# A hybrid decoder block: load order at the start, gate rows on ScalarE, selectors ahead, products of some pairs exchanged

## The chip, the cores and the metric

The kernel runs on one core of one Trainium2 chip. The metric is the device time of one execution in microseconds; the time of a kernel is the median of its runs. One execution is also taken by the hardware profiler, and all rows below are from it. Engines: PE is TensorE, DVE VectorE, ACT ScalarE, POOL GpSimd, and SP issues most of the transfers.

## The reference, cut to what matters

A block with 512 tokens and 16 meta tokens (528 columns, NT), 1024 channels, float32. Two mixers read the same normed input; learned gates merge them; a SwiGLU follows.

```
xn   = rmsnorm(h) * g1
proj = xn @ w_in           # mq mk mv mi mf mo | gq gk gv ga gr | gate_m gate_g
mq, mk = silu(causal conv of width 4)
hm   = mLSTM in chunks of 64, 4 heads: weights exp(b_t - b_s + i_s - m_t), from gates mi, mf
y_m  = headnorm(hm) * sigmoid(mo)
y_g  = headnorm(gated linear attention of gq gk gv) * silu(gr)
h   += (sigmoid(gate_m) * (y_m @ W_m) + sigmoid(gate_g) * (y_g @ W_g)) @ W_out
h   += (silu(hn @ Wfg) * (hn @ Wfu)) @ Wdown,   hn = rmsnorm(h) * g2
out  = rmsnorm(h) * gf
```

## The kernel before, in words

Everything lies transposed: channels on the 128 partitions, tokens in the columns. A *unit* is one block of 128 output channels: its weights, 128 x 1024 (512 KB), come from DRAM into a tile `raw` (4 buffers, L183) and are split into a high part on ScalarE (`whi`, L190) and the rest on VectorE (`wlo`, L195). x is split in the same way, and every product is three matmuls, high x high, high x low, low x high (`mm3`, L304 to L306). A unit is 8 k-steps over the input channels. Where it needs all 528 columns, a k-step is two halves of 264 columns, six matmuls.

The order of the work is the order in which the code is traced; each engine works through its own queue in that order. All small work is in Python generators. `run` puts one into the list `side`, `mix` into the list `mixers`; after each k-step `tick` takes each generator in `side` one step further, and of `mixers` the first alone. So the heads of the mLSTM run one after another, a head's generator begins where the one ahead ends, and `yield n` waits n ticks. PSUM has 8 banks, taken by `bank()`; a product into a bank waits until its last reader is done.

`begin` issues the load five units ahead, and it puts the splits of later units into the current one's k-steps by a table (PLAIN for a unit, FIRST and SECOND for a pair).

The order of units is: gates, mq 0; a sum of squares over all channels (L1091) and from it `rstd` (`rsqrt_mean`); mk 0, mv 0, mv 1, mo 0, mo 1, mq 1, mk 1, mv 2 and so on, 24 units to 191 us. Up to mv 1 products use x without its norm, and `rstd` is multiplied in where a bank is read. `normed_x` writes the normed x meanwhile.

`gate_rows` (L629) starts with the k-steps of mk 0. On 32 partitions it makes the log gates, running sums and maxima (a scan, L660), the four groups of rows `R`, and for each distance d of two chunks a row (ten adds with one scalar per partition, L685). These are transposed (L701) into a bank and copied to `acol` (L695), and then `ready` lets the heads of the mLSTM begin. A head (`mlstm`, L878) copies its selector (L883) and lets six ticks pass. Two products with `R` spread the head's rows over all partitions (L886 and the one before it). Then come scores, exponentials and weights for each chunk of keys.

From 191 us many units are taken as *pairs*: two blocks of outputs with x in quarters, seven products in place of eight (`pair`, L351). A pair forms seven products p7, q1, p3 (that of the pair before), q6, p4, p2, q5 of four k-steps each into three banks:

```
        seven(bz, w, x, "p7", True, hook, *cols)
        seven(bx, w, x, "q1", True, hook, *cols)
        if "p3" in pend:
            pend.pop("p3")(hook)
```

q1 and q6 go into the same bank, and between them the copy `s1` (L406 here, L1391 in the gate/up pairs) reads q1 from it; `s7` (L409) reads p7 from its bank. Both are issued at the first k-step of p3; where no p3 is pending, that is right behind q1. Such a pair follows single units: gm 0, gq 0, and the first of 16 gate/up pairs. `s2` adds two halves of a raw tile (L229) and releases it. A tick follows every second k-step of a pair.

At the end `final` (L1487) sums the squares of the outputs, takes Ln and Exp on ScalarE, refines the result on VectorE in four operations (L1501 to L1504) and scales the outputs.

Of the kernel before, what the change touches and what calls it, by code (L numbers as in the profile page):

```python
# [8 lines left out]
F32 = mybir.dt.float32  # L9
# [93 lines left out]
def hybrid_block(ctx: ExitStack, tc: tile.TileContext, xT, wst, par, con, out):  # L103
# [5 lines left out]
    def nm(s):  # L109
        cnt[0] += 1  # L110
        return f"{s}_{cnt[0]}"
# [86 lines left out]
    def split_hi(u):  # L198
        splits[u] = [whi(raws[u])]

    def split_lo(u):
        splits[u].append(wlo(raws.pop(u), splits[u][0]))
# [54 lines left out]
    def g_lo(u):  # L257
# [6 lines left out]

    PLAIN = {"s": [(split_hi, 2), (split_lo, 4)], "e": [(e_hi, 1), (e_lo, 3), (s2, 4)],
             "a": [(a_hi, 1), (a_lo, 3), (f_hi, 4), (s4, 5)]}
    FIRST = {"s": [(split_hi, ("q1", 2)), (split_lo, ("p3", 1))],
             "e": [(e_hi, ("q1", 2)), (e_lo, ("p3", 1)), (s2, ("q6", 1))]}
    SECOND = {"s": [(split_hi, ("p2", 0)), (split_lo, ("p2", 2))],
              "a": [(a_hi, ("p2", 0)), (a_lo, ("p2", 2)), (f_hi, ("q5", 0)), (s4, ("q5", 2))],  # L270
              "e": [(e_hi, ("p2", 0)), (e_lo, ("p2", 2)), (s2, ("q5", 2))]}
# [79 lines left out]
    def pair(names, x, cols, sink):  # L351


        u, steps = begin(*names)
        w = mixw[u].w
        bz, bx, by = (bank()[:, :cols[1] - cols[0]] for _ in range(3))
        e = sink(bz, bx, by)
        todo = {("p7", 0): ["s5"], ("p7", 2): ["mid", "c22"], ("q6", 0): ["c12"], ("q6", 2): ["fin"]}
        mine = {("p3", 0): ["s1", "s7"], ("p4", 0): ["s2"], ("p2", 1): ["c21"], ("q5", 0): ["c11"]}
        steps.setdefault(("p7", 3), []).append(lambda: f_lo(u))  # L360
        steps.setdefault(("q6", 1), []).append(lambda: g_hi(u))
        steps.setdefault(("p4", 1), []).append(lambda: g_lo(u))

        def hook(n, k):
            left(*todo.get((n, k), ()))
            for s in mine.get((n, k), ()):
                e.pop(s)()
            for f in steps.get((n, k), ()):
                f()
            if k % 2:  # L370
                tick()

        seven(bz, w, x, "p7", True, hook, *cols)
        seven(bx, w, x, "q1", True, hook, *cols)
        if "p3" in pend:
            pend.pop("p3")(hook)
        else:
            for k in range(4):
                hook("p3", k)
        seven(bx, w, x, "q6", False, hook, *cols)  # L380
        seven(bz, w, x, "p4", False, hook, *cols)
        seven(by, w, x, "p2", True, hook, *cols)
        seven(bx, w, x, "q5", False, hook, *cols)
        assert not pend, pend
        pend.update(e)
        pend["p3"] = lambda hook=lambda n, k: None: seven(bx, mixw.pop(u).w, x, "p3", False, hook, *cols)
# [29 lines left out]
        return sink  # L416


    pr = cpool.tile([P, NPAR], F32, name="pr")
    nc.sync.dma_start(pr[:, :C_A2], par[:, :C_A2])  # L420
    load_raw(0)
    xs = []
    for k in range(KT):
        t = tt()
        nc.sync.dma_start(t, xT[k])
        xs.append(t)
        if k == 3:
            load_raw(1)
    load_raw(2)
    nc.sync.dma_start(pr[:, C_A2:], par[:, C_A2:])  # L430
    ident = pr[:, C_ID:C_ID + P]
    ones = cpool.tile([P, P], F32, name="ones")
    G.memset(ones, 1.0)
    cb = cpool.tile([P, 4], F32, name="cb")
    G.memset(cb[:, 0:1], EPS)
    G.memset(cb[:, 1:2], 0.5 * math.log(QS2))
# [22 lines left out]
    for c in range(NCK):  # L459
        G.memset(rmask[:, CH * c:CH * c + 1], 0.0)  # L460

    split_hi(0)
    split_lo(0)
    ready[0] = 3


    xh, xl, sq = [], [], []
    for k in range(KT):
        g = pr[:, C_N1 + k:C_N1 + k + 1]
        hi = tt(F32R)  # L470
        act(hi, xs[k], AF.Copy, scale=g)
        lo = tt(F32R)
        V.scalar_tensor_tensor(lo, xs[k], g, hi.bitcast(F32), ALU.mult, ALU.subtract)  # L473
        xh.append(hi)
        xl.append(lo)
        if k == 5:
            split_hi(1)
            split_lo(1)
    xsum = tt()
    for k in range(KT):  # L480
        sq = xsum if k == 0 else tt()
        act(sq, xs[k], AF.Square)
        if k > 0:
            V.tensor_tensor(xsum, xsum, sq, ALU.add)
    split_hi(2)
    split_lo(2)
    load_raw(4)
    onesr = cpool.tile([P, P], F32R, name="onesr")
    S.copy(onesr, ones)
# [136 lines left out]
    gts = Box()  # L626
    gts.ready = False

    def gate_rows(ps):  # L629
        a2s = gts.a2s = apool.tile([P, 512], F32R, name="a2s")  # L630
        a2f = pr[:, C_A2:C_A2 + 512]
        gsb = tt()
        for a in range(2):
            c = slice(a * HALF, (a + 1) * HALF)
            V.tensor_tensor(gsb[:96, c], ps[0][a][:96], rstd[:96, c], ALU.mult)
        yield 16
        gam = gts.gam = tt(F32R)
        S.copy(gam[:96], gsb[:96])
        bi = pr[0:32, C_BG:C_BG + 1]
        bf = pr[32:64, C_BG:C_BG + 1]  # L640
        r1, r2, bl, a0 = tt(p=32), tt(p=32), tt(p=32), tt(p=32)
        act(r1, gsb[32:64], AF.Abs, bias=bf)
        yield 1
        act(r1, r1, AF.Exp, scale=-1.0)
        V.tensor_scalar(r2, gsb[32:64], bf, 0.0, op0=ALU.add, op1=ALU.min)
        yield 1
        act(r1, r1, AF.Ln, bias=b_one[:32])
        V.tensor_tensor(gam[64:96], gsb[64:96], gam[64:96].bitcast(F32), ALU.subtract)
        S.copy(a2s[:96], a2f[:96])
        yield 1  # L650
        V.tensor_tensor(r2, r2, r1, ALU.subtract)
        V.tensor_tensor_scan(bl, rmask[:32], r2, 0.0, ALU.mult, ALU.add)
        yield 1
        V.tensor_tensor(a2s[32:64], a2f[32:64], a2s[32:64].bitcast(F32), ALU.subtract)
        V.scalar_tensor_tensor(a0, gsb[0:32], bi, bl, ALU.add, ALU.subtract)
        yield 1
        d0, ml = r1, r2
        V.memset(d0, 0.0)
        V.tensor_copy(d0[:, CH::CH], bl[:, CH - 1:NT - 1:CH])
        V.tensor_tensor_scan(ml, d0, a0, 0.0, ALU.add, ALU.max)  # L660
        yield 1
        R = gts.R = tt(F32R, NS)
        mr = tt(p=32)
        rhi = d0
        act(R[0:32], ml[:, NM:], AF.Copy, scale=-1.0)
        V.tensor_tensor(mr, ml, bl, ALU.add)
        V.tensor_scalar(mr, mr, -1.0, 40.0, op0=ALU.mult, op1=ALU.min)
        yield 1
        V.scalar_tensor_tensor(R[32:64], ml[:, NM:], -1.0, R[0:32].bitcast(F32), ALU.mult, ALU.subtract)
        S.copy(R[64:96], mr[:, NM:])  # L670
        yield 1
        S.copy(rhi[:, NM:], R[64:96].bitcast(F32))
        yield 1
        V.tensor_tensor(R[96:128], mr[:, NM:], rhi[:, NM:], ALU.subtract)

        acol = gts.acol = apool.tile([P, 480], F32, name="acol")
        gts.idx = {}
        rows = [a0]
        n_ix = 0
        for d in range(NCK):  # L680
            if d > 0:
                nxt = tt(p=32)
                for i in range(NCK - d):
                    e = CH * (i + d) - 1
                    V.tensor_scalar(nxt[:, CH * i:CH * i + CH], rows[-1][:, CH * i:CH * i + CH], bl[:, e:e + 1],  # L685
                                    None, op0=ALU.add)
                rows.append(nxt)
            yield 2
        yield 8
        pst = bank()  # L690
        for d in range(NCK):
            n_ix = gate_cols(pst, rows, d, n_ix)
            yield 1
        yield 2
        V.tensor_copy(acol, pst[:, :480])  # L695
        gts.ready = True

    def gate_cols(pst, rows, d, n_ix):
# [176 lines left out]
    WTOT = off  # L875


    def mlstm(h, q, k, v, gates, dst):  # L878
        while not gts.ready or q.v is None or k.v is None:
            yield 1  # L880
        (qh, ql), (kh, kl) = q.v, k.v
        sel = mpool.tile([P, 2, P], F32R, tag="sel", name=nm("sel"))
        S.copy(sel, cn[:, NS + h:NS + 8:H].unsqueeze(2).to_broadcast([P, 2, P]))  # L883
        yield 6
        pb, pm = bank(), bank()
        T.matmul(pb, sel[:, 0], gts.R, start=True, stop=True)  # L886
        T.matmul(pm, sel[:, 1], gts.R, start=True, stop=True)
        yield 1
        nml, dia, em = tt(n=NS), tt(n=NS), tt(n=NS)
        S.copy(nml, pb)  # L890
        V.tensor_tensor(dia, pb, mask, ALU.add)
# [194 lines left out]
    X.neg = [xdram.tile([2, P, HA], F32, tag="neg", name=nm("neg")) for _ in range(4)]  # L1086
    ps_g = unit_all(("gates", 0))
    ps_q = unit_all(("mq", 0))[0]
    ps_ss = [bank()[:, :HALF], bank()[:, :HALF]]
    for a in range(2):  # L1090
        T.matmul(ps_ss[a], ones, xsum[:, a * HALF:(a + 1) * HALF], start=True, stop=True)  # L1091
# [87 lines left out]
    for job in JOBS[2:]:  # L1179
# [27 lines left out]
        elif what == "mk":  # L1207
            b = head("m", i)
            if i == 0:
                b.src = [box(), box()]  # L1210
                run(conv(b.src[0], (ps_q, rstd), 0, False))
                run(gate_rows(ps_g))
            run(conv(b.src[1], unit_all(job[0]), 4 + i, True))
            run(conv_act(b.q, b.k, b.src))
        elif what == "mv":
# [271 lines left out]
    def final(a, o):  # L1487
# [6 lines left out]
        yield 1  # L1494
        T.matmul(ps, ones, hsum[a].w, start=False, stop=True)
        yield 1
        y, t = tt(n=HS), tt(n=HS)
        act(y, ps, AF.Ln, bias=b_eps, scale=1.0 / D)
        act(y, y, AF.Exp, scale=-0.5)
        yield 1  # L1500
        V.tensor_tensor(t, y, y, ALU.mult)  # L1501
        V.scalar_tensor_tensor(t, ps, D * EPS, t, ALU.add, ALU.mult)
        V.tensor_scalar(t, t, -0.5 / D, 1.5, op0=ALU.mult, op1=ALU.add)
        V.tensor_tensor(y, y, t, ALU.mult)  # L1504
        yield 1
        for j in range(4):
            g = hgain[j, a]
# [114 lines left out]
```

## Time and profile before

| what | value |
|---|---|
| median of 3 runs | 942.75 us (942.73 to 942.78) |
| profiled execution, its own time | 943.2 us |
| its span, first to last instruction | 941.1 us |
| TensorE busy | 917.7 us, 98% |
| VectorE, ScalarE, GpSimd busy | 641.0, 536.7, 86.5 us |
| mean granted clock of TensorE | 0.993 |

Busy time is that in which an instruction runs; a busy TensorE may still run at a low clock, which the granted clock (1.0 is full) shows. A row of a timeline gives start and length in us and, in brackets, the time that the engine was idle before it and what ended that. L134 is the line of the helper for all activations, so its rows are told apart by shape and place.

### The profile page before, as it was taken

What the parts mean: (1) busy time and instruction counts of PE and PEld (TensorE: products, weight loads), DVE (VectorE), ACT (ScalarE), POOL (GpSimd) and SP (SyncE); (2) the same over time, 40 slices, a digit from 0 to 9 for tenths busy, and PEclk for the clock granted to TensorE, in tenths of its full rate; (3) what the DMA queues carried; (4) which work ended last, traced back from release to release, by engine and by line L of the source; (5) the groups of instructions that cost most, each with busy time, mean ns of one, the idle gap of its engine ahead of it and who ended that gap; (6) DMA issues with size and microseconds to landing.
All of it is one profiled execution on the core that took longest, in us unless ns stands there. A gap on an engine that the chain in (4) does not pass through costs nothing.

```text
span 941.1 us, 15476 instructions
## 1 busy us (share of the span) xinstructions
PE 917.7 (98%) x6083; PEld 843.0 (90%) x6083; DVE 641.0 (68%) x948; ACT 536.7 (57%) x947; POOL 86.5 (9%) x102
## 2 busy tenths in 40 slices
PE   6999999989999999999999999999999999999995
PEld 6989999989998899999998888888999999888885
DVE  6898776877865477777777556886767677832323
ACT  7556678779674266767774234443555555732321
POOL 0000022011100011111000000212111210000000
PEclk9999999999999999999999999999999999999998
DMA  6345465355752466565553344244887775332302
GB/s 255 111 132 164 136 141 134 71 125 123 173 143 88 114 152 163 135 139 141 134 137 90 114 141 131 86 124 116 196 187 186 190 179 148 113 108 70 112 1 89
DMA packets 48713, 124.45 MB, mean 132 GB/s; under 512 B 5377, under 2 KB 11521, under 8 KB 48641
## 3 DMA queue, kind: packets, MB, share of 16 engines
q1 hardware_dynamic: 35008, 101.32, 34.6%
q0 software_dynamic: 12544, 21.11, 14.5%
q8 instruction: 47, 0.77, 0.3%
q10 hardware_dynamic: 1088, 1.05, 0.3%
q14 instruction: 26, 0.20, 0.1%
HBM read 118.08 MB, written 5.37 MB: 131 GB/s over the span
## 4 chain that ended last, share of the span: by engine, by line
PE 88%; DVE 5%; ACT 5%; issue 1%; DMA 1%; SPq 0%; DVEq 0%; ACTq 0%
PE b L305 14%; PE b L304 14%; PE b L306 14%; PE b L346 12%; PE b L348 12%; PE b L347 12%; ACT t L134 2%; ACT whi L190 1%; DVE wlo L195 1%; PE b L1069 1%; PE b L1071 1%; PE b L1048 1%; DMA t<-xT 1%; PE b L753 1%; PE b L951 1%
## 5 line engine op out<-in xcount | busy, mean ns | idle before, releaser
L305 PE MATMUL b<-t,whi 128*128 128x512 f32 (+2 forms) x822 | 290.8, 354 | 1.1 <-DVE t L473 0.7
L304 PE MATMUL b<-t,whi 128*128 128x512 f32 (+2 forms) x774 | 274.6, 355 | 6.6 <-ACT t L134 6.6
L306 PE MATMUL b<-t,wlo 128*128 128x512 f32 (+2 forms) x774 | 271.6, 351 | 0.0
L346 PE MATMUL b<-t,whi 128*128 128x256 f32 (+1 forms) x864 | 249.6, 289 | 3.5 <-ACT t L406 2.8
L348 PE MATMUL b<-t,wlo 128*128 128x256 f32 (+1 forms) x864 | 245.3, 284 | 0.0
L347 PE MATMUL b<-t,whi 128*128 128x256 f32 (+1 forms) x864 | 244.5, 283 | 0.0
L195 DVE TENSOR_TENSOR wlo<-raw,whi 128x1024 fp32r<-128x1024 f32 x155 | 193.3, 1250 | 46.2 <-ACT whi L190 45.5
L190 ACT CAST whi<-raw 128x1024 fp32r<-128x1024 f32 x155 | 161.4, 1045 | 62.3 <-PE b L347 26.0
L305 PEld LDWEIGHTS b<-t,whi 128*128 128x128 f32 x822 | 156.4, 190 | 23.7 <-DVE t L473 1.3
L304 PEld LDWEIGHTS b<-t,whi 128*128 128x128 f32 x774 | 147.7, 191 | 26.6 <-ACT t L134 6.6
L346 PEld LDWEIGHTS b<-t,whi 128*128 128x128 f32 x864 | 164.0, 190 | 5.3 <-ACT t L406 3.8
L306 PEld LDWEIGHTS b<-t,wlo 128*128 128x128 f32 x774 | 147.3, 190 | 19.9 <-DVE wlo L195 0.3
L347 PEld LDWEIGHTS b<-t,whi 128*128 128x128 f32 x864 | 163.9, 190 | 0.4
L348 PEld LDWEIGHTS b<-t,wlo 128*128 128x128 f32 x864 | 163.7, 189 | 0.0
L134 ACT ACTIVATE t<-t 128x512 f32<-128x512 f32 (+6 forms) x140 | 80.5, 593 | 58.9 <-DVE t L1098 27.7
L185 POOL DMA_DIRECT2D raw<-wst x36 | 31.1, 864 | 358.2 <-DMA wf<-wst 86.6
L190 ACT CAST whi<-wf 128x1024 fp32r<-128x1024 f32 x36 | 37.8, 1051 | 22.6 <-PE b L347 13.5
L134 ACT ACTIVATE t<-f 128x256 f32<-128x256 f32 (+1 forms) x24 | 11.6, 482 | 61.9 <-DVE f L1469 61.9
L214 POOL DMA_DIRECT2D wf<-wst x36 | 32.1, 901 | 157.2 <-DMA wf<-wst 116.0
L195 DVE TENSOR_TENSOR wlo<-wf,whi 128x1024 fp32r<-128x1024 f32 x36 | 43.8, 1218 | 0.0
L1469 DVE TENSOR_TENSOR f<-f,b 128x512 f32<-128x512 f32 (+1 forms) x9 | 5.6, 628 | 53.6 <-PE b L306 53.6
L346 PE MATMUL b<-t,wgh 128*128 128x256 f32 (+1 forms) x144 | 40.9, 284 | 0.0
(221 smaller groups left out, 1200.6 us busy)
## 6 DMA issues: line engine op xcount, KB each, us to landing
raw<-wst SPq DMA_DIRECT2D x155, 512.0 KB, 3.7
wf<-wst SPq DMA_DIRECT2D x36, 256.0 KB, 3.2
wf<-wst POOLq DMA_DIRECT2D x36, 256.0 KB, 5.6
raw<-wst POOLq DMA_DIRECT2D x36, 256.0 KB, 4.8
t<-xT SPq DMA_DIRECT2D x8, 264.0 KB, 6.1
pos<-t SPq DMA_DIRECT2D x8, 264.0 KB, 2.5
t<-xT SPq DMA_DIRECT2D x8, 256.0 KB, 3.9
t<-neg POOLq DMA_DIRECT2D x6, 272.0 KB, 6.3
```

The costliest lines, as they stand in the source:

```text
L134: S.activation(o, i, func, **kw)
L185: G.dma_start(lr(r, 0), lr(wst[v - 1], 0), accum_op=ALU.add)
L190: S.copy(t, src)
L195: V.tensor_tensor(t, src, hi.bitcast(F32), ALU.subtract)
L214: G.dma_start(lr(st.f, 1), lr(wst[u + 1], 1), accum_op=ALU.add)
L304: T.matmul(o, w_h, ah[:, c0:c1], start=first, stop=False)
L305: T.matmul(o, w_h, al[:, c0:c1], start=False, stop=False)
L306: T.matmul(o, w_l, ah[:, c0:c1], start=False, stop=last)
L346: T.matmul(o, h, xh_[k][:, c0:c1], start=start and k == 0, stop=False, skip_group_check=not start)
L347: T.matmul(o, h, xl_[k][:, c0:c1], start=False, stop=False, skip_group_check=not start)
L348: T.matmul(o, l, xh_[k][:, c0:c1], start=False, stop=k == 3, skip_group_check=not start)
L753: T.transpose(pb[:, c * P:(c + 1) * P], f[:, c * CH:(c + 1) * CH], ident)
```

## The change

At the start, `par` is loaded by ScalarE's queue. The first unit's weights are loaded and split in two halves, the first ahead of x, the second behind two tiles of x; raw 1 is loaded behind all of x. TensorE gets ten fp32 products of a constant tile with itself ahead of the first unit. The split of unit 1 is issued behind all parts of x, that of unit 2 inside the squares and their sum.

The gates' two banks are copied to SBUF by ScalarE behind unit mq 0, and `rstd` is multiplied in there in one operation. In `gate_rows` the memset goes to GpSimd and into a tile of its own, the ten row adds go to ScalarE as activations with a bias, and so does the copy to `acol`. The selector of head 0 is made in `gate_rows`, that of each next head behind the two products of the head before, and the six ticks fall away.

In FIRST the split of later weights is issued at p3 (steps 0 and 3) in place of q1 and p3, and `s2` a step later. A pair without a pending p3 computes q1 ahead of p7. In `final` one operand of the refinement is prepared beside Ln and Exp, and the chain behind Exp has three operations in place of four.

```diff
-    FIRST = {"s": [(split_hi, ("q1", 2)), (split_lo, ("p3", 1))],
-             "e": [(e_hi, ("q1", 2)), (e_lo, ("p3", 1)), (s2, ("q6", 1))]}
+    FIRST = {"s": [(split_hi, ("p3", 0)), (split_lo, ("p3", 3))],
+             "e": [(e_hi, ("p3", 0)), (e_lo, ("p3", 3)), (s2, ("q6", 2))]}
...
-        seven(bz, w, x, "p7", True, hook, *cols)
-        seven(bx, w, x, "q1", True, hook, *cols)
+        for b, n in ((bz, "p7"), (bx, "q1")) if "p3" in pend else ((bx, "q1"), (bz, "p7")):
+            seven(b, w, x, n, True, hook, *cols)
...
+    ones = cpool.tile([P, P], F32, name="ones")
+    G.memset(ones, 1.0)
     pr = cpool.tile([P, NPAR], F32, name="pr")
-    nc.sync.dma_start(pr[:, :C_A2], par[:, :C_A2])
-    load_raw(0)
...
+    S.dma_start(pr[:, :C_A2], par[:, :C_A2])
+    raws[0] = wpool.tile([P, D], F32, tag="raw", name=nm("raw"), bufs=4)
+    n_raw[0] = 1
+    nc.sync.dma_start(lr(raws[0], 0), lr(wst[0], 0))
+    load_x()
+    load_x()
+    nc.sync.dma_start(lr(raws[0], 1), lr(wst[0], 1))
+    while len(xs) < KT:
+        load_x()
     load_raw(2)
     nc.sync.dma_start(pr[:, C_A2:], par[:, C_A2:])
+
+    idle = bank()
+    for _ in range(10):
+        T.matmul(idle[:, :P], ones, ones, start=True, stop=True)
+    del idle
...
+    def first_half(j):
+        h, l = (lr(t, j) for t in splits[0])
+        S.copy(h, lr(raws[0], j))
+        V.tensor_tensor(l, lr(raws[0], j), h.bitcast(F32), ALU.subtract)
...
+    first_half(0)
+    x_parts()
+    x_parts()
+    first_half(1)
+    del raws[0]
+    while len(xh) < KT:
+        x_parts()
+    split_hi(1)
+    split_lo(1)
+    sq = [None] * KT
     for k in range(KT):
...
+        sq[k] = tt()
+        act(sq[k], xs[k], AF.Square)
         if k == 5:
-            split_hi(1)
-            split_lo(1)
...
+            split_hi(2)
+    xsum = sq[0]
+    for k in range(1, KT):
+        V.tensor_tensor(xsum, xsum, sq[k], ALU.add)
+        sq[k] = None
+        if k == 5:
+            split_lo(2)
...
-    def gate_rows(ps):
+    def gate_rows(gsb):
...
-        gsb = tt()
-        for a in range(2):
-            c = slice(a * HALF, (a + 1) * HALF)
-            V.tensor_tensor(gsb[:96, c], ps[0][a][:96], rstd[:96, c], ALU.mult)
+        V.tensor_tensor(gsb[:96], gsb[:96], rstd[:96], ALU.mult)
...
-        d0, ml = r1, r2
-        V.memset(d0, 0.0)
+        d0, ml = tt(p=32), r2
+        G.memset(d0, 0.0)
...
         V.tensor_tensor(R[96:128], mr[:, NM:], rhi[:, NM:], ALU.subtract)
+        selector(0)
...
-                    V.tensor_scalar(nxt[:, CH * i:CH * i + CH], rows[-1][:, CH * i:CH * i + CH], bl[:, e:e + 1],
-                                    None, op0=ALU.add)
+                    act(nxt[:, CH * i:CH * i + CH], rows[-1][:, CH * i:CH * i + CH], AF.Identity,
+                        bias=bl[:, e:e + 1])
...
-        V.tensor_copy(acol, pst[:, :480])
+        S.copy(acol, pst[:, :480])
...
+    def selector(h):
+        gts.sel = mpool.tile([P, 2, P], F32R, tag="sel", name=nm("sel"), bufs=1)
+        S.copy(gts.sel, cn[:, NS + h:NS + 8:H].unsqueeze(2).to_broadcast([P, 2, P]))
...
-        sel = mpool.tile([P, 2, P], F32R, tag="sel", name=nm("sel"))
-        S.copy(sel, cn[:, NS + h:NS + 8:H].unsqueeze(2).to_broadcast([P, 2, P]))
-        yield 6
+        sel = gts.sel
...
+        if h < H - 1:
+            selector(h + 1)
...
     ps_q = unit_all(("mq", 0))[0]
+
+    gsb = tt()
+    for a in range(2):
+        S.copy(gsb[:96, a * HALF:(a + 1) * HALF], ps_g[0][a][:96])
+    del ps_g
...
         act(y, ps, AF.Ln, bias=b_eps, scale=1.0 / D)
+        V.tensor_scalar(x, ps, D * EPS, -0.5 / D, op0=ALU.add, op1=ALU.mult)
         act(y, y, AF.Exp, scale=-0.5)
         yield 1
         V.tensor_tensor(t, y, y, ALU.mult)
-        V.scalar_tensor_tensor(t, ps, D * EPS, t, ALU.add, ALU.mult)
-        V.tensor_scalar(t, t, -0.5 / D, 1.5, op0=ALU.mult, op1=ALU.add)
-        V.tensor_tensor(y, y, t, ALU.mult)
+        V.tensor_tensor(t, t, x, ALU.mult)
+        V.scalar_tensor_tensor(y, t, 1.5, y, ALU.add, ALU.mult)
```

## Rows read from the trace of the kernel before

**Rows 1.** Page, part 4: the chain that ended last, by engine.
```profile
PE 88%; DVE 5%; ACT 5%; issue 1%; DMA 1%; SPq 0%; DVEq 0%; ACTq 0%
```
**Rows 2.** TensorE's waits: who for whom, us in total, times, longest.
```profile
PE b L304 <- ACT t L134: 6.6, 1, 6.6
PE b L346 <- ACT t L406: 2.8, 2, 2.3
PE b L886 <- ACT sel L883: 2.2, 1, 2.2
...
PE b L346 <- ACT t L1391: 0.5, 1, 0.5
```
**Rows 3.** Windows: us; PE, PEld, DVE, ACT, POOL; PEclk, DMA share, GB/s.
```profile
71.00:75.00 4.00, 4.00 (x20) 3.91 (x20) 4.00 (x8) 0.44 (x2) 0.00 (x0) 0.57 0.53 166
211.00:215.00 4.00, 4.00 (x22) 4.00 (x22) 3.56 (x7) 3.63 (x8) 0.87 (x1) 0.57 0.56 111
8.00:10.00 2.00, 2.00 (x9) 2.00 (x10) 1.81 (x3) 1.48 (x3) 0.00 (x0) 1.00 0.99 388
```
**Rows 4.** ScalarE's timeline, 10 to 23 us: start, busy, work, idle before.
```profile
10.68 1.41 ACT L134 ACTIVATE t<-t,pr 128x528 fp32r<-128x528 f32 x2 [1.20 <-DMA t<-xT]
...
14.19 4.37 ACT L134 ACTIVATE t<-t 128x528 f32<-128x528 f32 x8
```
**Rows 5.** VectorE's timeline, 15 us, and a group of the page's part 5.
```profile
15.56 5.57 DVE L484 TENSOR_TENSOR t<-t,t 128x528 f32<-128x528 f32 x7
...
L195 DVE TENSOR_TENSOR wlo<-raw,whi 128x1024 fp32r<-128x1024 f32 x155 | 193.3, 1250 | 46.2 <-ACT whi L190 45.5
```
**Rows 6.** TensorE's timeline, 22 to 24 us.
```profile
22.26 1.05 PE L1091 MATMUL b<-t,ones 128*128 128x264 f32 x4
22.96 0.48 PE L304 MATMUL b<-t,whi 128*128 128x264 f32 x1
23.28 0.28 PE L305 MATMUL b<-t,whi 128*128 128x264 f32 x1
23.40 0.28 PE L306 MATMUL b<-t,wlo 128*128 128x264 f32 x1
```
**Rows 7.** VectorE's timeline, 49 to 70 us.
```profile
49.85 0.50 DVE L658 MEMSET t<- 32x528 f32 x1
...
63.35 1.27 DVE L617 TENSOR_TENSOR t<-b,t 128x512 f32<-128x512 f32 x2
...
69.30 0.65 DVE L695 COPY acol<-b 128x480 f32<-128x480 f32 x1
```
**Rows 8.** ScalarE's timeline, 195 us: three exponentials.
```profile
195.55 1.00 ACT L134 ACTIVATE t<-t,acol 128x112 f32<-128x112 f32 x3
```
**Rows 9.** ScalarE's timeline, 54 to 56 us.
```profile
54.34 1.05 ACT L190 CAST whi<-raw 128x1024 fp32r<-128x1024 f32 x1
...
55.83 0.43 ACT L134 ACTIVATE t<-t 128x272 f32<-128x272 f32 x1
```
**Rows 10.** TensorE's timeline, 56 us: transposes of gate rows.
```profile
56.51 0.57 PE L701 MATMUL b<-pr,t 32*128 32x32 f32 x4
```
**Rows 11.** TensorE's timeline, 210 us: the second pair.
```profile
209.86 0.39 PE L346 MATMUL b<-t,whi 128*128 128x256 f32 x1 [2.32 <-ACT t L406]
```
**Rows 12.** ScalarE's timeline, 208 to 210 us.
```profile
208.22 1.03 ACT L190 CAST whi<-raw 128x1024 fp32r<-128x1024 f32 x1
...
209.46 0.35 ACT L406 COPY t<-b 128x256 f32<-128x256 f32 x1
```
**Rows 13.** Line L886, one of two selector products: count, ns, first and last.
```profile
L886 PE MATMUL b<-t,sel x4: 396/398/499, 70.7 to 192.6; 128*128 128x512 f32 x4
```
**Rows 14.** VectorE's timeline, the tail.
```profile
934.16 0.29 DVE L1503 TENSOR_SCALAR t<-t 128x256 f32<-128x256 f32 x1
```
**Rows 15.** Timeline of SP in a pair, and page part 6.
```profile
699.89 0.33 SPq L183 DMA_DIRECT2D raw<-wst  x1
...
raw<-wst SPq DMA_DIRECT2D x155, 512.0 KB, 3.7
```

More of the change, by code (lines that the diff above doesn't have):

```diff
@@ L416, in sink_of, with load_x @@
         return sink
+    ones = cpool.tile([P, P], F32, name="ones")
+    G.memset(ones, 1.0)
     pr = cpool.tile([P, NPAR], F32, name="pr")
-    nc.sync.dma_start(pr[:, :C_A2], par[:, :C_A2])
-    load_raw(0)
     xs = []
-    for k in range(KT):
+    def load_x():
         t = tt()
-        nc.sync.dma_start(t, xT[k])
+        nc.sync.dma_start(t, xT[len(xs)])
         xs.append(t)
-        if k == 3:
-            load_raw(1)
+    S.dma_start(pr[:, :C_A2], par[:, :C_A2])
[7 more added lines that the diff above has]
+        load_x()
     load_raw(2)
     nc.sync.dma_start(pr[:, C_A2:], par[:, C_A2:])
+    idle = bank()
+    for _ in range(10):
+        T.matmul(idle[:, :P], ones, ones, start=True, stop=True)
+    del idle
     ident = pr[:, C_ID:C_ID + P]
-    ones = cpool.tile([P, P], F32, name="ones")
-    G.memset(ones, 1.0)
     cb = cpool.tile([P, 4], F32, name="cb")
@@ L460, in hybrid_block, with x_parts @@
         G.memset(rmask[:, CH * c:CH * c + 1], 0.0)
-    split_hi(0)
-    split_lo(0)
     ready[0] = 3
-    xh, xl, sq = [], [], []
-    for k in range(KT):
[L469 to L475, printed above, removed]
-        if k == 5:
-            split_hi(1)
-            split_lo(1)
[L479 to L486, printed above, removed]
+    xh, xl = [], []
+    splits[0] = [wpool.tile([P, D], F32R, tag="w" + s, name=nm("w" + s), bufs=4) for s in ("hi", "lo")]
+    def first_half(j):
+        h, l = (lr(t, j) for t in splits[0])
+        S.copy(h, lr(raws[0], j))
+        V.tensor_tensor(l, lr(raws[0], j), h.bitcast(F32), ALU.subtract)
+    def x_parts():
+        k = len(xh)
+        g = pr[:, C_N1 + k:C_N1 + k + 1]
+        xh.append(tt(F32R))
+        xl.append(tt(F32R))
+        act(xh[k], xs[k], AF.Copy, scale=g)
+        V.scalar_tensor_tensor(xl[k], xs[k], g, xh[k].bitcast(F32), ALU.mult, ALU.subtract)
+    first_half(0)
[8 more added lines that the diff above has]
+    sq = [None] * KT
+    for k in range(KT):
+        sq[k] = tt()
+        act(sq[k], xs[k], AF.Square)
+        if k == 5:
+            split_hi(2)
[5 more added lines that the diff above has]
+            split_lo(2)
+    del sq
     load_raw(4)
@@ L888, in mlstm @@
         yield 1
+        del sel
+        if h < H - 1:
+            selector(h + 1)
         nml, dia, em = tt(n=NS), tt(n=NS), tt(n=NS)
@@ L1211, in hybrid_block @@
                 run(conv(b.src[0], (ps_q, rstd), 0, False))
-                run(gate_rows(ps_g))
+                run(gate_rows(gsb))
             run(conv(b.src[1], unit_all(job[0]), 4 + i, True))
@@ L1496, in final @@
         yield 1
-        y, t = tt(n=HS), tt(n=HS)
+        y, t, x = tt(n=HS), tt(n=HS), tt(n=HS)
         act(y, ps, AF.Ln, bias=b_eps, scale=1.0 / D)
+        V.tensor_scalar(x, ps, D * EPS, -0.5 / D, op0=ALU.add, op1=ALU.mult)
         act(y, y, AF.Exp, scale=-0.5)
```

## The prediction

> **What bounds the kernel now.** I read four views, in this order. The chain that ended last comes first: 88% of the span is TensorE, so what matters is where TensorE stands still and where it runs slowly [rows 1]. The list of TensorE's waits gives the first: 6.6 us before its first product, 2.2 us for the selector of mLSTM head 0, 2.3 + 0.5 us in pairs for a ScalarE copy (L406), 0.5 us for the same copy in the gate/up pairs (L1391) [rows 2]. All the rest of the span but the tail is uninterrupted products. The stretches of the clock give the second: two 4-us stretches have a mean granted clock of 0.57, one behind the wait at 70.7 us, one behind the wait at 209.9 us [rows 3]. At full clock each would have passed 4 x 0.43 = 1.7 us of work more. So the waits of 2.2 and 2.3 us really cost 3.9 and 4.0 us; the waits of 0.5 us have no such stretch behind them. The timelines of ScalarE and VectorE then say why each wait ends late. The sum is made against the profiled execution: 943.2 us, span 941.1, 2.1 us around it; the median 942.75 lies 0.45 lower.
>
> **The start.** The load order gives x 512 KB less ahead of it (raw 1 goes behind x) and one issue less on SP (par goes to ScalarE's queue; 0.33 us [rows 15]). At 388 GB/s 512 KB are 1.3 us [rows 3]. The fifth x tile landed at 10.68 us [rows 4]; three more of 264 KB at 0.7 us each give 12.7 for the last, now 11.1. Its high part ends at 11.8 instead of 14.2 us, where the squares begin today [rows 4]. But the split of unit 1 moves behind all x parts: raw 1 lands at 12.4, the whi copy takes to 13.4, wlo to 14.6 (1.05 and 1.25 us each [rows 5, 9]). Unit 1 (mq 0) is 48 products with starts 0.12 us apart [rows 6] and then ends 5.8 us later, at 20.4. xsum needs seven adds, 5.57 us [rows 5], and now has wlo 2 (1.2 us) inside it: 14.6 + 5.6 + 1.2 = 21.4. So the sum over x waits about 1.0 us; its own products took 0.7 us (22.26 to 22.96), and unit 2, which starts at 22.96 today [rows 6], starts at 22.1: TensorE leads by 0.9 us, no more. The ten constant products (fp32, before x) can only help the clock during the first 8 us, where x's arrival is the limit; I book nothing, at most 0.6 us either way. On ScalarE the squares start 0.9 us earlier, but two copies of the gate rows (about 0.35 us each) now stand ahead of the table load for Ln: rstd comes within 0.2 us of today. The bounds are 1.2 us earlier (if the 1.2 us that ScalarE idled for x falls away [rows 4]) and 0.5 us later.
>
> **Gate rows and selector.** From rstd to 70 us VectorE and ScalarE run one chain behind TensorE; the lead counts only if this chain keeps up. It gains 0.5 us by the memset that goes to GpSimd [rows 7]. The ten row adds (L685) go from VectorE to ScalarE. ScalarE has not run this form; the nearest rows are exponentials of 112 and 128 columns, three in 1.0 us, so I take 0.3 us each, 3.0 in all (bounds 0.2 and 0.6) [rows 8]. By their ticks they come behind the copies of 54.3 to 56.2 us: the first four end at 56.2 - 0.5 + 0.3 (selector 0) + 1.2 = 57.2 us [rows 9]. TensorE's transposes of these rows stand at 56.51 today [rows 10], so the lead of 0.9 is used up and 0.7 us more is lost. VectorE is relieved of 10 adds, but waits for ScalarE: L762 needs a ScalarE copy that has been pushed behind the adds; L617 after it moves from 63.35 to 63.7 [rows 7].
> Selector 0 is now ready at 54 us, so the wait of 2.2 us for it goes, and the two products that use it come six ticks (six k-steps of six products, 4.3 us) earlier: TensorE came to them at 70.7 - 2.2 = 68.5, so 64.2 and the 0.7 us lost, some 65 us [rows 2, 13]. What is late next is a PSUM bank: at the start of mv 2, the unit in whose k-steps this falls, the unit before it (2), its own first half, the selector products (2), the gate columns, the transposed values and the first score product hold all eight. I expect 0.7 us for L617 to release one, 0.6 us for the conv evacuation, and at the start of mv 2 about 1.9 us in two pieces for acol (now on ScalarE behind its queue, 71.4 us) and for the copy of the product itself (72.3). In today's trace acol ran at 69.30 [rows 7]. Then mv 2 goes on at 72.7 where it went on at 71.3 today, but at full clock and with the score products of three key chunks done instead of one: 0.7 us by the clock's end at 75, and 0.9 us when the next unit starts. I take -0.9 us for all up to 80 us. The bounds are -4.8 (lead 0.9 and wait 3.9 all kept) and +2.
>
> **Pairs.** In FIRST the whi copy moves from ("q1", 2) to ("p3", 0), which is behind s1 and s7. At the second pair the order on ScalarE was: L134, whi 208.22 (1.03), L134, s1 at 209.46, and TensorE went on at 209.86 [rows 11, 12]. Without that whi ahead s1 comes 0.9 us earlier: 2.3 becomes 1.4. More goes by another edit: each head's mLSTM starts six ticks earlier (no yield of 6 behind the selector) and the heads run one after another. So head 3, whose selector products are at 192.6 today [rows 13], comes up to 24 ticks, 18 us, earlier; its exponentials then no longer stand ahead of s1 in the second pair. I take the whole wait with its slow clock: -2.3 - 1.7 = -4.0 us. Bounds: -0.9 and -4.0.
> Where no p3 is pending (first pair after single units), q1 now goes ahead of p7, so s1 copies q1 during p7's 1.4 us. The waits before q6, 0.5 us at 333 and 0.5 us at 650 [rows 2], go: -1.0. Weights of q1 are needed 1.4 us earlier, but their splits are done before the pair begins. In the other pairs, which wait nowhere, the order of products is as it was; wlo and s2 are later by one or two k-steps, behind whi, which costs nothing while raw tiles still land in time (rival 5).
>
> **Tail.** One VectorE operation leaves the chain after the last sum, L1503, 0.29 us [rows 14]; its replacement runs beside Ln and Exp: -0.3 us.
>
> Sum: -0.9 - 4.0 - 1.0 - 0.3 = -6.2 us: 937.0 for such a profiled execution, 936.6 for the median.
>
> **The rivals.**
> 1. The banks come free in time and all of the 68.5-us wait is won: -4.8 in place of -0.9, 932.7 us. For it: VectorE loses 3.4 us of work in 50 to 70 us. Against it: ScalarE gets as much in the same chain. 0.10.
> 2. The wait at 68.5 us comes back in pieces and the clock falls again: 1.7 us more, 938.3 us. For it: I count four waits for banks there, the longest 1.9 us in two pieces. Against it: single waits of 0.5 us left the clock alone. 0.15. (The Trainium skill, "TensorE: Matmul & The Clock Gate", section "A second HAM failure mode: psum-queue depth-cycling", says that small pauses between groups of products, as PSUM banks are cycled, can already make the clock fall and rise. By that rule this rival is the forecast. The trace before shows falls behind single long waits alone and so does not settle it.)
> 3. The second pair keeps 1.4 us and its slow clock, since head 2's and 3's work is still ahead of s1: -0.9 in place of -4.0, 939.7 us. For it: the ScalarE queue there waits for VectorE, which earlier heads don't change by themselves. 0.14.
> 4. The gains cancel: head 3's mLSTM, 18 us earlier, falls into 175 to 190 us and delays the copies for the first pair by a wait of the 4.0-us kind, and rival 2 holds as well: -6.2 + 4.0 + 1.7 = -0.5, 942.3 us; the waits have moved and the change doesn't do what it says. 0.12.
> 5. Slower. In the steady pairs s2 releases a raw tile, and SP loads the next into it at once (699.89) [rows 15]. Now whi and wlo run between q1's evacuation and s2, so the load starts about 3 us later. If the split two pairs on then waits, each of the 36 pairs pays. 0.25 us each is 9 us: 945.5. It decides as soon as a tile lands later than its copy is due; a load lands 3.7 us after its issue [rows 15], and from issue to that copy I count some 13 us. 0.09.
>
> **How the numbers follow.** Forecast 0.40, rivals 0.10, 0.15, 0.14, 0.12, 0.09. A measurement here tells 0.2% (1.9 us) from no change. Faster: forecast and rivals 1 to 3, 0.79; same: rival 4, 0.12; slower: rival 5, 0.09. The forecast's own range is 935.0 to 938.2. For 8 in 10 the range starts at rival 1's 932.8 and goes past rival 3 (938.2 to 940.9, by the +2 bound of the first stage) to 941.5.
>
> **What would show it.** TensorE's waits: none for the selector; for L406 and L1391 none, or under 0.5 us. Granted clock: no stretch at half after 13 us but the tail. Unit 2 starts near 22.1, the transposes of the gate rows at 57, and the first TensorE waits lie between 56 and 73 us, on ScalarE's row adds and on evacuations. The last selector products are near 174 us. L1503's place in the tail is empty. It is wrong if a clock stretch at half remains, if a wait over 1 us appears after 80 us, or if unit 2 starts no earlier than today.

## The result, and the profile after

The kernel became slower: 949.2 us (median of 4 runs, 948.13 to 950.84) against 942.76 us; ratio 1.0069, 95% interval 1.0051 to 1.0086. The forecast was 936.6 us. The profiled execution took 950.07 us, its span is 948.3 us, 7.2 us more than before.

Page of the kernel after, the first line of its part 4:

```profile
PE 86%; ACT 6%; DVE 5%; issue 1%; DMA 1%; SPq 0%; DVEq 0%; ACTq 0%
```

TensorE is still the chain, but ScalarE has 6% of it, a point more than in [rows 1]. TensorE's waits in the kernel after (who for whom, us in total, times, longest):

```profile
PE b L346 <- ACT t L407: 5.2, 1, 5.2
PE b L346 <- ACT t L408: 2.1, 1, 2.1
PE b L304 <- ACT t L134: 2.0, 2, 1.6
```

Against [rows 2] the wait for the selector and the wait of 2.3 us are gone. In their place stand two longer ones: 5.2 us for s1 (L407 of the kernel after) and 2.1 us for s2 (L408). TensorE's timeline puts the first in the first pair (gm 0), where q6 waits for s1, and the second in the third pair, where a later product into the same bank waits for s2:

```profile
203.42 0.58 PE L346 MATMUL b<-t,whi 128*128 128x256 f32 x1 [5.20 <-ACT t L407]
...
238.66 0.53 PE L346 MATMUL b<-t,whi 128*128 128x272 f32 x1 [2.14 <-ACT t L408]
```

Windows of the kernel after (columns as in [rows 3]; the column before the last two is the granted clock):

```profile
201.00:208.00 7.00, 4.58 (x21) 4.59 (x22) 4.73 (x9) 4.98 (x10) 1.72 (x2) 0.52 0.46 81
208.00:215.00 7.00, 7.00 (x54) 6.74 (x53) 2.74 (x5) 2.90 (x4) 0.00 (x0) 1.00 0.62 181
238.50:242.50 4.00, 3.83 (x18) 3.84 (x19) 4.00 (x8) 2.82 (x7) 0.00 (x0) 0.57 0.29 99
```

Behind the first wait the granted clock is 0.52 for seven microseconds, nearly all of it the lower of the two levels (1.2 of 2.4 GHz): 7 x 0.48 = 3.4 us lost. Behind the second it is as in [rows 3], 4 x 0.43 = 1.7 us. So the two waits cost 5.2 + 3.4 + 2.1 + 1.7 = 12.4 us, and two waits of 0.3 us stand beside them: 13.1 us in this execution. The stretch from 191 to 300 us had cost 2.3 + 1.7 = 4.0 us before; the difference is +9.1 us.

That this is the place is seen at one copy that both kernels make, s1 of the seventh pair. First before, then after:

```profile
270.01 0.37 ACT L406 COPY t<-b 128x256 f32<-128x256 f32 x1
```

```profile
278.21 0.37 ACT L407 COPY t<-b 128x256 f32<-128x256 f32 x1 [1.04 <-PE b L348]
```

It is 8.2 us late, so the kernel had been about 0.9 us ahead at the first pair (8.2 - 9.1; a remainder, which no row shows by itself). Nothing is lost behind it. Why s1 came late, ScalarE's timeline of the kernel after tells:

```profile
189.69 1.28 ACT L133 ACT_TABLE_LOAD   x1
...
191.52 0.51 ACT L950 CAST wh<-t 128x400 fp32r<-128x400 f32 x1
...
200.02 0.31 ACT L950 CAST wh<-t 128x144 fp32r<-128x144 f32 x1 [2.19 <-DVE t L946]
200.24 0.37 ACT L800 CAST t<-b 128x256 fp32r<-128x256 f32 x1
200.62 1.28 ACT L133 ACT_TABLE_LOAD   x1
201.91 1.09 ACT L134 ACTIVATE t<-b 128x512 f32<-128x512 f32 x2
202.88 0.21 ACT L950 CAST wh<-t 128x16 fp32r<-128x16 f32 x1
202.98 0.39 ACT L407 COPY t<-b 128x256 f32<-128x256 f32 x1
```

L950 copies the weights of head 3's mLSTM, chunk by chunk. They stand ahead of s1 in ScalarE's queue, and ScalarE idles 2.19 us in front of one of them, for a product that VectorE makes (L946). The two rows of 1.28 and 1.09 us behind it are a table load for the activations and the two Tanh of the gates mo 6 and 7. VectorE's timeline shows the product L946 behind head 2's normalisation (L858, L865), a weight sum (L241) and the low part of head 3's values (L788):

```profile
195.44 0.69 DVE L858 SCALAR_TENSOR_TENSOR t<-t,t 128x512 f32<-128x512 f32 x1
...
197.06 0.69 DVE L241 TENSOR_TENSOR wg<-wf,raw 128x512 f32<-128x512 f32 x1
...
199.02 0.69 DVE L788 TENSOR_TENSOR t<-b,t 128x512 fp32r<-128x512 f32 x1
199.62 0.31 DVE L946 TENSOR_TENSOR t<-b,t 128x144 f32<-128x144 f32 x1
```

The selector line names the head (count, ns, first and last start):

```profile
L914 PE MATMUL b<-t,sel x4: 394/398/484, 62.8 to 175.7; 128*128 128x512 f32 x4
```

Head 3's selector products start at 175.7 us, where [rows 13] has 192.6: 17 us earlier, so its chain of exponentials and weight copies now ends in the first pair. What s1 copies had long been computed: the last product of q1 in that pair starts at 195.94 us, and s1 starts at 202.98.

```profile
195.94 0.28 PE L348 MATMUL b<-t,wlo 128*128 128x256 f32 x1
```

In the kernel before, one exponential of head 3 stood just ahead of s1 of the first pair, and s1 began 0.4 us behind the end of q1 (194.63 us):

```profile
194.45 0.70 ACT L134 ACTIVATE t<-b,cb 128x512 f32<-128x512 f32 x1
195.04 0.37 ACT L406 COPY t<-b 128x256 f32<-128x256 f32 x1
```

### The profile page after: what moved, and what is told of

Read it like the earlier page. It is cut to its first block, busy times and chain, and to the rows that moved or that the text cites. A ratio compares the mean times of both kernels' runs of the same rounds, so it can differ in the third digit from the quotient of the medians.

```text
span 948.3 us, 15513 instructions
## 1 busy us (share of the span) xinstructions
PE 922.7 (97%) x6103; PEld 846.2 (89%) x6103; DVE 637.6 (67%) x936; ACT 538.5 (57%) x960; POOL 87.4 (9%) x103
## 3 DMA queue, kind: packets, MB, share of 16 engines
q10 hardware_dynamic: 1232, 1.09, 0.3%
## 4 chain that ended last, share of the span: by engine, by line
PE 86%; ACT 6%; DVE 5%; issue 1%; DMA 1%; SPq 0%; DVEq 0%; ACTq 0%
PE b L304 14%; PE b L305 14%; PE b L306 14%; PE b L346 12%; PE b L348 12%; PE b L347 12%; ACT t L134 2%; ACT whi L190 1%; DVE wlo L195 1%; PE b L1100 1%; ACT L133 1%; PE b L1102 1%; PE b L1079 1%; DMA raw<-wst 1%; PE b L982 1%
## 5 line engine op out<-in xcount | busy, mean ns | idle before, releaser
L195 DVE TENSOR_TENSOR wlo<-raw,whi 128x1024 fp32r<-128x1024 f32 x154 | 193.3, 1258 | 99.7 <-ACT whi L190 99.4
L134 ACT ACTIVATE t<-t 128x512 f32<-128x512 f32 (+5 forms) x140 | 80.6, 595 | 58.9 <-DVE t L1134 27.6
L214 POOL DMA_DIRECT2D wf<-wst x36 | 35.2, 978 | 151.1 <-DMA wf<-wst 80.4
L195 DVE TENSOR_TENSOR wlo<-wf,whi 128x1024 fp32r<-128x1024 f32 x36 | 43.9, 1219 | 0.0
L1505 DVE TENSOR_TENSOR f<-f,b 128x512 f32<-128x512 f32 (+1 forms) x9 | 5.7, 629 | 54.0 <-PE b L306 54.0
L1427 ACT COPY t<-b 128x256 f32<-128x256 f32 x48 | 16.4, 375 | 43.8 <-PE b L348 43.8
```

Of the source, the lines that this page charges most:

```text
L134: S.activation(o, i, func, **kw)
L195: V.tensor_tensor(t, src, hi.bitcast(F32), ALU.subtract)
L214: G.dma_start(lr(st.f, 1), lr(wst[u + 1], 1), accum_op=ALU.add)
L1427: s7=lambda: S.copy(s[:, lo], bz), s1=lambda: S.copy(s[:, hi], bx), s2=lambda: S.copy(r[:, lo], bx),
```

## The experiments

Two theories stood at first. **A, early heads:** without its six ticks every head starts earlier than the one before allowed, head 3 by 17 us, and its ScalarE and VectorE chain stands ahead of s1 in the first pair. **B, late splits:** the new table FIRST makes s1 and s2 late. All times are medians beside the kernel before on the same chip (942.7 us), with the ratio and its 95% interval.

**The six ticks back in every head.**

```diff
         sel = gts.sel
+        yield 6
```

> The kernel after, with the six ticks back between the selector and its two products, in every head. Theory A (early heads: head 3's mLSTM came 17 us earlier, into the first pair, where its ScalarE and VectorE chain makes s1 late): the waits of 5.2 and 2.1 us and the clock that falls behind them (3.4 and 1.7 us) go; the wait of 2.3 us with its 1.7 us may return in the second pair. 949.2 - 12.4 = 936.8, or 940.8 with the old wait. Theory B (the later splits in FIRST make s1 and s2 late): no change from 949.2, within 1 us.

Measured: 939.14 us, ratio 0.9966 (0.9954 to 0.9977). The waits from 60 us to the last of the early pairs:

```profile
PE b L916 <- ACT acol L721: 1.5, 1, 1.5
PE b L346 <- ACT t L407: 1.4, 1, 1.4
...
PE b L346 <- ACT t L408: 0.4, 1, 0.4
```

Ten microseconds come back with one line. The wait for s1 is back in the second pair at 1.4 us, with a slow clock behind it.

**FIRST as before.**

```diff
+    FIRST = {"s": [(split_hi, ("q1", 2)), (split_lo, ("p3", 1))],
+             "e": [(e_hi, ("q1", 2)), (e_lo, ("p3", 1)), (s2, ("q6", 1))]}
```

> The kernel after, with the table FIRST of before (split at q1 step 2 and p3 step 1, s2 at q6 step 1). Theory A (early heads): the heads stand as in the kernel after, so the waits in the first pair and near 238 us stay: 949.2, and up to 1 us more, since a split of 1.05 us stands ahead of s1 again. Theory B (FIRST): the time returns to 936 to 941 us.

Measured: 948.63 us, ratio 1.0064 (1.0049 to 1.0079). Theory B is out: the wait for s1 of the first pair is there, and is 6.1 us.

```profile
PE b L346 <- ACT t L407: 7.2, 2, 6.1
```

**Selectors ahead and no six ticks, alone, on the kernel before.**

```diff
-        yield 6
+        sel = gts.sel
...
+        if h < H - 1:
+            selector(h + 1)
```

> The kernel before, with one part of the change alone: selectors made ahead, and no six ticks in a head. Theory A (early heads): the loss in the pairs comes with this part alone, +8 to +9 us, and at 68 us the wait of 2.2 us for the selector turns into others: 942.8 + 6 to 9 = 949 to 952. Theory B (FIRST): the pairs are as in before, so 942.8 less up to 3.9 us from the wait at 68.5 us: 939 to 943.

Measured: 950.39 us, ratio 1.0084 (1.0067 to 1.01). TensorE's waits from 190 us on have the same 6 us:

```profile
PE b L346 <- ACT t L406: 7.1, 2, 6.1
PE b L346 <- ACT t L407: 1.2, 1, 1.2
```

This part alone carries the whole loss, with the pairs and the start of before.

**Only the last head late.**

```diff
         sel = gts.sel
+        if h == H - 1:
+            yield 24
```

> The kernel after, with 24 ticks of waiting in front of the last head's two products alone, so that this head stands where it stood before and heads 0 to 2 stay early. Theory A in the form that head 3 alone is to blame: as with six ticks in every head, 936.8 to 940.8. If head 2's work, 12 us earlier, is what delays s1 as well: 941 to 949. Theory B (FIRST): 949.2, within 1 us.

Measured: 938.34 us, ratio 0.9955 (0.994 to 0.997). All of TensorE's waits of 190 to 335 us are now one line:

```profile
PE b L346 <- ACT t L407: 1.0, 2, 0.6
```

Heads 0 to 2 may be early; head 3 alone did the harm. The second pair's wait, 2.3 us before, is 0.4 us, and the granted clock there is not lowered.

**Half of that delay.**

```diff
+        if h == H - 1:
+            yield 12
```

> The kernel after, with 12 ticks (some 8.5 us) of waiting in front of the last head's two products, half of what puts that head where it stood before. If the loss falls evenly with the delay: halfway between 949.2 and 938.3, near 944. If it is a collision of the head's exponentials with s1 of the first pair, the delay moves the collision: the exponentials then run at 185 to 212 us, s1 of the first pair still has two or three of them ahead of it, and s1 of the second pair is close behind them: 941 to 950.

Measured: 942.64 us, ratio 1.0002 (0.9993 to 1.0011). TensorE's waits of 190 to 335 us:

```profile
PE b L346 <- ACT t L408: 2.4, 1, 2.4
PE b L346 <- ACT t L407: 1.2, 2, 0.9
```

12 ticks already free s1 of the first pair (0.9 us there). What stays is the other wait, for s2 of the third pair, and a slow clock behind it. ScalarE's timeline shows what stands ahead of that s2:

```profile
225.83 1.28 ACT L133 ACT_TABLE_LOAD   x1
227.12 0.74 ACT L134 ACTIVATE t<-t,cb 128x528 f32<-128x528 f32 x1
...
228.66 1.28 ACT L133 ACT_TABLE_LOAD   x1
229.95 1.15 ACT L134 ACTIVATE t<-t 128x512 f32<-128x512 f32 x2
231.01 0.36 ACT L408 COPY t<-b 128x272 f32<-128x272 f32 x1
```

These are the logarithm of the first linear-attention head and, behind a second table load, the two Tanh of the gates gm 2 and 3 from the pair ahead. They stand ahead of s2 with the last head 24 ticks late as well, where no such wait is left. That TensorE then has head 3's own products to do between the pair's would fit; no run separates it. The gains are 6.6 us for the first 12 ticks and 4.3 us for the next; the medians alone are only 1.2 us from an even fall (943.8). The waits show that it is a matter of place: the first pair's went nearly whole, the third pair's stayed.

**The two Tanh ahead of s1 moved behind it, head 3 early.**

```diff
+        if wait:
+            yield wait
...
+            run(gates_of(boxes, held.pop(what), func, 6 if i == 7 else 0))
```

> The kernel after, with six ticks of waiting in front of the two Tanh of the last mLSTM gates (mo 6 and 7), so that they and the table load ahead of them come behind s1 of the first pair. Theory A1 (s1 is late because it stands in ScalarE's queue behind head 3's chain and these): 1.28 + 1.09 = 2.4 us less in front of s1, the wait of 5.2 becomes 2.8 us, and half of the slow clock behind it (1.7 us) may go: 945 to 947. Theory A2 (the time is lost because TensorE has none of head 3's products left between the pairs' own, whatever stands in front of s1): within 1 us of 949.2. The two banks are held for six ticks more; a new wait for a bank would show as a wait on these Tanh.

Measured: 947.17 us, ratio 1.0051 (1.0036 to 1.0067), 2.0 us less than the kernel after. By the medians that is not clear of noise (945.74 to 949.18 here, 948.13 to 950.84 there); what follows rests on the trace. TensorE's wait, ScalarE's timeline and the window behind:

```profile
PE b L346 <- ACT t L407: 3.7, 1, 3.7
```

```profile
199.57 0.31 ACT L952 CAST wh<-t 128x144 fp32r<-128x144 f32 x1 [2.19 <-DVE t L948]
...
200.89 0.20 ACT L952 CAST wh<-t 128x16 fp32r<-128x16 f32 x1 [0.73 <-DVE t L948]
201.00 0.36 ACT L407 COPY t<-b 128x256 f32<-128x256 f32 x1
```

```profile
200.00:207.00 7.00, 5.58 (x34) 5.46 (x35) 5.62 (x12) 6.24 (x12) 1.72 (x2) 0.76 0.56 113
```

s1 starts 2.0 us earlier, of which TensorE itself was 0.5 us earlier, and TensorE's wait is 3.7 us in place of 5.2 (A1 had forecast 2.8): the place in ScalarE's queue is part of the cause. The rest stays, since ScalarE waits for VectorE all the same; the 2.19 us of idling are unchanged. The slow stretch behind it is half as long (7 x 0.24 = 1.7 us lost). So 1.5 of the 5.2 us are the Tanh and their table load; the other part is the chain between the two engines, by its place in these rows, and no run took it apart further. Theory A2 can explain little of it: in the kernel before, three score products of head 3 stand between q1 and q6 of this pair (from 194.47 us, with q6 at 195.46), so an estimate from these rows is that they hid about 1 us.

**The start alone, on the kernel before.** The lines of the start (halves, load order, constant products, order of squares and splits) are those of the change; all else is as before.

> The kernel before, with the start of the change alone: halves of the first weights ahead of x, par on ScalarE's queue, constant products, order of squares and splits. If the lead of 0.4 us at mk 0 that the kernel after shows is kept to the end: 942.4. If the chain of the gate rows does not follow and the wait for the selector takes it: 942.8. More than 1 us faster would say that the start reaches further than mk 0 shows.

Measured: 941.91 us, ratio 0.9993 (0.9984 to 1.0002). The expectation misread the lead: unit 2 starts at 21.90 us in the kernel after and at 22.96 before, 1.1 us. The wait for the selector stays 2.2 us, and the product that waits starts at 69.90 us (70.74 before), so a lead of 0.8 us is not eaten by it; but 0.8 us can't be told from none by the medians.

```profile
69.90 0.50 PE L913 MATMUL b<-t,sel 128*128 128x512 f32 x1 [2.21 <-ACT sel L910]
```

**Without the constant products** (last head late).

```diff
-    for _ in range(10):
-        T.matmul(idle[:, :P], ones, ones, start=True, stop=True)
```

> The kernel after with its last head 24 ticks later (938.3), without the ten constant products. The prediction's step (x's arrival limits the first 8 us, they are worth 0 and at most 0.6 us): 938.3, to 938.9. Rival: the granted clock then rises near 13 us in place of 4 to 7 us, and the products of the first unit behind x are slower: 1 to 2 us, 939.3 to 940.3.

Measured: 937.86 us, ratio 0.9952 (0.9939 to 0.9964), against 0.9955 with them. They are worth nothing, as booked. They do bring the faster clock sooner: without them the first unit's products start 0.22 us apart until 10.4 us and 0.12 us apart behind it, with them 0.12 us apart from 6.6 us. But unit 2 starts at 21.41 us without and at 21.67 with them; in both it stands behind the sum over x, which waits for VectorE (0.69 and 0.60 us).

**Row adds on VectorE again** (last head late).

```diff
-                    act(nxt[:, CH * i:CH * i + CH], rows[-1][:, CH * i:CH * i + CH], AF.Identity,
-                        bias=bl[:, e:e + 1])
+                    V.tensor_scalar(nxt[:, CH * i:CH * i + CH], rows[-1][:, CH * i:CH * i + CH], bl[:, e:e + 1],
+                                    None, op0=ALU.add)
```

> The kernel after with its last head 24 ticks later (938.3), with the ten row adds on VectorE again. The prediction's step (on ScalarE they delay the transposes by 0.4 us and the copies behind them, on VectorE they cost 10 x 0.27 us of the chain that frees banks at 63 to 72 us): the wait of 0.4 us at the transposes goes, waits at 63 to 72 us grow by up to 1 us: 938 to 939.5. Rival: the adds are better on VectorE, the wait of 1.6 us at 71.6 us shrinks: 936.5 to 937.5.

Measured: 938.28 us, ratio 0.9952 (0.994 to 0.9965): no difference. The wait at the transposes shrinks from 0.4 to 0.15 us, the one of 1.6 us at 71 us stays.

**The pairs of before** (last head late): FIRST and the order p7, q1 as before.

> The kernel after with its last head 24 ticks later (938.3), with the pairs of before: the old table FIRST, and p7 ahead of q1 in every pair. The prediction's step for the pairs: the waits of 0.5 us at the first pair behind the bm units and at the first gate/up pair return (+1.0), and a split of 1.05 us stands ahead of s1 in the second pair again, so its wait of 0.4 us becomes 1.3 us, with a slow clock behind it (+1.7) or without: 940.2 to 941.9. Rival: the pair edits are worth nothing, 938.3 within 0.4.

Measured: 942.15 us, ratio 0.9998 (0.9988 to 1.0007), 3.8 us more than with the new pairs. TensorE's waits of 190 to 335 us:

```profile
PE b L346 <- ACT t L407: 4.0, 5, 1.4
```

That is 3.0 us more than with the new pairs, in the first four pairs (0.74, 0.77, 0.62 and 1.38 us) and the one behind the bm units (0.52), and there are 0.5 us more at the first gate/up pair. The wait of 1.3 us that was expected in the second pair is 0.77, with no slow clock; more pairs wait than were named, and the time lies 0.2 us above the range. The pair edits are what pays in this change, as soon as head 3 is out of their way; which of the two edits pays, this run does not separate.

**Selectors ahead, last head late, on the kernel before.**

```diff
         sel = gts.sel
+        if h == H - 1:
+            yield 24
```

> The kernel before with selectors ahead and no six ticks (950.4 alone), and the last head 24 ticks later. Theory A (early head 3): the loss goes, and what stays is the gate stage (waits of 2.2 us and 1.7 us of slow clock against 1.7 us of waits and perhaps 1.7 us of clock) and the second pair with head 2 earlier (its wait of 2.3 us shrinks to 1.3, with or without 1.7 us): 939 to 942.

Measured: 941.41 us, ratio 0.9988 (0.9979 to 0.9998). Nine microseconds less than the same kernel with head 3 early.

**The three together:** last head late, no constant products, row adds on VectorE.

> The kernel after with its last head 24 ticks later, without constant products, and with the row adds on VectorE: each of the two was within 0.5 us of 938.3. If they add up: 937.5, within 0.7.

Measured: 937.41 us, ratio 0.9947 (0.9932 to 0.9962). It beats both kernels; that it beats 938.34 can't be told.

## Why the prediction was wrong

**The step that failed is the pairs.** It said that head 3 "comes up to 24 ticks, 18 us, earlier; its exponentials then no longer stand ahead of s1 in the second pair", and took "the whole wait with its slow clock: -4.0 us". The first half is measured (17 us, and the second pair's wait went). What the step left out is that the same chain had to go somewhere: 17 us earlier, its end is in the first pair. There only one of its exponentials had stood ahead of s1 before; now the end of the chain stands there, with ScalarE's idling for VectorE in it, and makes a wait more than twice as long. The term was -4.0 us; it is +9.1 us. The mechanism stood in rival 4, "falls into 175 to 190 us and delays the copies for the first pair", with a chance of 0.12. Its place was right; its price, one wait of the 4.0-us kind, was too small by a factor of two for s1 alone (5.2 + 3.4), and it did not see s2 of the third pair (2.1 + 1.7). It was priced from the length of another wait, not by following the chain through both queues at 185 to 203 us. Two of the prediction's own signs of being wrong came: a stretch at half clock, and a wait over 1 us behind 80 us.

**The price of the clock** was taken as a part of each long wait (2.2 and 2.3 us "really cost 3.9 and 4.0"). With the start alone the same wait for the selector, 2.21 us, has no slow stretch behind it:

```profile
71.00:75.00 4.00, 3.88 (x30) 3.54 (x29) 3.61 (x8) 0.69 (x1) 0.00 (x0) 1.00 0.54 187
```

So 1.7 of these 3.9 us are of that one execution, and the gain that the gate stage could have is smaller than the bound of -4.8 says.

**The start** was right in TensorE's lead (0.9 us booked, 1.1 measured). Its timeline of the kernel after:

```profile
21.10 1.16 PE L1127 MATMUL b<-t,ones 128*128 128x264 f32 x4 [0.60 <-DVE t L510]
21.90 0.48 PE L304 MATMUL b<-t,whi 128*128 128x264 f32 x1
```

Unit 2 starts at 21.90 us (forecast 22.1, before 22.96), and the sum over x has the wait that was named, 0.6 us of the 1.0 forecast.

**The gate stage** fits in sum: -0.9 us was forecast up to 80 us, and the remainder above gives some 0.9 us at the first pair. That is no test of the parts, since that remainder also holds a new wait of 0.6 us between 80 and 190 us and the clock of the execution before. The ten row adds took 3.02 us on ScalarE, 0.30 each as taken:

```profile
55.47 3.02 ACT L134 ACTIVATE t<-t,t 32x128 f32<-32x128 f32 x10
```

The waits came where they were named and a little shorter: 0.4 us at the transposes, 0.56 us for the bank that L617 (now L645) reads, 0.24 us for the conv evacuation, 1.6 us at 71.9 us for a ScalarE activation that frees a bank (forecast 1.9, for copies).

**The other pair starts:** the two waits of 0.5 us are gone, as forecast. That q1's splits "are done before the pair begins" did not hold in the first pair: TensorE waits 0.35 us there for the low weights of q1 (L195, at 194.79 us). The split out of s1's way and the new order were booked at 0.9 and 1.0 us; with head 3 late they are worth 3.8. (The pair behind the bm units is gq 1; the list of such pairs ahead of the prediction should name it, not gq 0.) **The tail:** its chain is shorter by the one operation; from the last VectorE operation ahead of it (L1469, now L1505) to the scaling of the outputs behind it (L1508, now L1544) it takes 4.0 us in place of 4.3, but from there to the end of the span 0.7 us more passed in that execution.

Rival 5 did not come: from 330 to 645 us the kernels run in parallel, and s2 a few steps later costs nothing. Rival 3's remaining 1.4 us appeared with the six ticks back in each head, where the heads stand about as before, which fits the 0.9 us taken for the split. With the last head late that wait is 0.4 us: heads 0 to 2 are early there, but head 3 also stands 3.5 us later (its selector products at 194.6 against 191.1 us), and no run separates the two.

## What to carry to other kernels

A chain that is moved earlier must be followed to its new place: list what the queues of both engines hold there, and which evacuation stands behind it, before its old wait is booked as a gain. In ScalarE's queue an idle wait for VectorE (2.19 us here) delayed everything behind it, so copies that a matmul waits for are better kept away from a two-engine chain; another engine for them was not tried here. Where the start of a side job is set by waiting a fixed number of steps, sweep that number: here one line decides between 949.2 and 938.3 us.

## What the runs showed of the hardware

The clock did not answer to the same waits in the same way. Up to 170 us the kernel after, the one with FIRST as before and the one with the last head late issue the same work. Windows 55 to 63 and 70 to 78 us, first of FIRST as before, then of the last head late:

```profile
55.00:63.00 8.00, 7.42 (x41) 6.08 (x40) 5.50 (x8) 6.62 (x18) 0.00 (x0) 0.79 0.57 183
70.00:78.00 8.00, 6.40 (x51) 6.19 (x51) 6.70 (x13) 6.20 (x16) 0.00 (x0) 1.00 0.38 119
```

```profile
55.00:63.00 8.00, 7.38 (x50) 5.93 (x48) 5.50 (x8) 6.62 (x17) 0.00 (x0) 1.00 0.59 180
70.00:78.00 8.00, 6.40 (x39) 6.35 (x39) 6.70 (x13) 6.20 (x15) 0.00 (x0) 0.79 0.32 119
```

In one execution the clock is lowered in the first stretch, in the other in the second, and in the kernel after in neither (1.00 in both). So behind waits of 0.2 to 1.6 us between products the clock fell in some executions and not in others: rival 2 is an event of a single execution. The Trainium skill, "TensorE: Matmul & The Clock Gate", section "A second HAM failure mode: psum-queue depth-cycling", names short pauses that come back as PSUM banks are cycled as a cause of the clock falling and rising. These rows agree that the clock can fall there; but it falls once, for 8 x 0.21 = 1.7 us of lost work, and does not swing to and fro.

The loss can be larger, and part of it can come back. Without the constant products the same window shows

```profile
55.00:63.00 8.00, 7.53 (x39) 6.37 (x39) 5.49 (x8) 6.62 (x17) 0.00 (x0) 0.71 0.59 177
```

that is 8 x 0.29 = 2.3 us of lost work, and 4 x 0.28 = 1.1 us more in the four microseconds behind. But TensorE's waits at 63 to 72 us, 0.6 + 0.2 + 1.6 us with the constant products, are 0.2 us in all there: that fits work which, coming later, found its banks free, and the median is no longer (937.86 against 938.34 us).

Waits of about 2 us are no different. Behind the selector wait of 2.21 us above, and behind a wait of 2.13 us for s2 of the third pair (at 236.09 us with the two Tanh late), the clock stayed up:

```profile
235.00:240.00 5.00, 3.52 (x26) 3.30 (x26) 4.96 (x9) 3.83 (x9) 0.00 (x0) 1.00 0.37 111
```

The same two waits had 1.7 us of slow clock behind them in the kernel before and in the kernel after. Behind the wait of 3.7 us 1.7 us were lost, behind the one of 5.2 us 3.4 us, and 3.4 us also behind the one of 6.1 us with FIRST as before. The four executions of the kernel after have mean granted clocks of 0.988 to 0.995, the slowest the lowest: such falls are part of why one kernel's times spread by 1 to 3 us.
